# Top-k search of the sparse-attention indexer: whole-number keys for both halves, one chain per query block, bounds of two blocks kept on ScalarE

## The chip, the core and the metric

The kernel runs on one core of one Trainium2 chip. The metric is the device time of one execution in microseconds, the median of several runs. The core's engines are TensorE (PE; PEld is its weight load), VectorE (DVE), ScalarE (ACT), GpSimd (POOL) and SyncE (SP, which issues the DMAs). Each has a queue of its own and works through it in order.

## What is computed

One layer of a decoder trunk over 1024 tokens of width 1024: an embedding norm, two self-attentions side by side (a sliding window of 128, and a sparse attention that lets each query see 256 chosen keys), an output projection, cross-attention to 256 memory tokens and a squared-ReLU feed-forward. The part that matters here is the choice of keys:

```python
dots = jnp.einsum('bqhd,bsd->bqhs', iqb, ik, preferred_element_type=jnp.float32) * (IDX_DIM ** -0.5)
score = jnp.einsum('bqh,bqhs->bqs', iwb.astype(jnp.float32), jax.nn.relu(dots))
causal = key_pos[None, :] <= t[:, None]
score = jnp.where(causal[None], score, NEG_INF)
_, idx = lax.top_k(score, topk)          # topk = 256
```

Ties go to the lowest index. Queries come in blocks of 128, one to a partition; block n has (n + 1) * 128 causal keys, so blocks 0 and 1 take all of theirs and only the six blocks 2 to 7 are searched.

## The kernel before, in words

Matmuls split each fp32 operand into a high and a low part and add three products (`mm3`, L102; every matmul is recorded at L86). The program is written in phases, but a planner sets the order of each engine's queue when the kernel is built, from its own estimates of time, and that order is then fixed. The stretch of this case is phase 1:

- **Scores** (`index_scores`, L572). For each index head and block PE makes the products, ACT applies the relu (L585), DVE adds them up in `sc` (L592). After the last head POOL copies the high 16 bits of each score to `hi_k` (L594).
- **Search** (L606 to L741). The 256th largest score of each query is found bit by bit: 15 bits of the high half (L715), then 16 of the low half among the scores that share the high half (L730). In each bit the keys at or above a bound are counted, and the bound moves. For blocks 2 to 5 DVE counts (`count`, L638, with an accumulator), and its small steps on the four bounds go together as 128x4 (L672, L677 for a high bit; L697, L698, L699 for a low one). For blocks 6 and 7 ACT sums the signs of key minus bound (`sign_sum`, L641, L642), and DVE moves the bound by small 128x1 steps: L668, L672, L677 for a high bit, L692, L693 for a low one. High bounds are bit patterns in int32, compared as bf16; low bounds are whole numbers in fp32. `lo_k` (L711, on POOL) and L718 to L729 (on DVE) stand between the halves.
- **Masks** (L742 to L751). For each block five passes on DVE turn the scores into a mask of 0 and -1e30.
- **Fill** (`fill`, L490 to L550, issued from L754). Beside the search PE makes the projections of queries and keys and the keys and values of the memory tokens. ACT empties the PSUM banks (L393, L456, L465, L487); weights come in by DMA to the ring `wr`, ACT, DVE or POOL make the high part (L160, L158, L156), POOL or DVE the low part (L161). The last units are `mem_v` (two products for each of four heads; ACT L465, then DVE L466) and `mem_vo`.

Phase 2 (attention) needs the fill's results; its first step on DVE that PE waits for in each unit is the split of the transposed probabilities (L783). After that come the output projection, cross-attention and the feed-forward, which the change doesn't touch.

Of the kernel before, what the change touches and what calls it, by code (L numbers as in the profile page):

```python
# [34 lines left out]
def kernel(ctx: ExitStack, tc: tile.TileContext, x, mem, ln_emb_g, ln_emb_b, w_in, b_in,  # L35
# [395 lines left out]
    # memory keys, and memory values taken through the output projection  # L431
# [86 lines left out]
    def first_loads(i):  # L518
        """The first heads' operands, a part at a time, each behind the last load of weights."""
# [52 lines left out]
    def index_scores(j, qs):  # L572
        for e in range(2):
            h = 2 * j + e
            for n in (2, 4, 6, 3, 5, 7):
# [17 lines left out]
                if h == 7:  # L593
                    POOL.tensor_scalar(hi_half(n), halves(n, 1), 1.0, 0.0, op0=OP.mult, op1=OP.add)  # L594
# [23 lines left out]
    h16 = p1.tile([P, NQ], F32)
    base = p1.tile([P, NQ], F32)
    need = p1.tile([P, NQ], F32)  # L620
    t_lo = p1.tile([P, NQ], F32)
    thr = p1.tile([P, NQ], I32)
    junk = {e: p1.tile([P, 1024], BF, name="junk" + e, tag="r", bufs=3) for e in "va"}
    lo_k = {}
    for tag, bufs, ns in (("ikh", 1, (7, 6)), ("ikl", 1, (5, 4, 3)), ("qs", 4, (2,))):
        t = p1.tile([P, sum(n + 1 for n in ns) * P], U16, name="lo_k", tag=tag, bufs=bufs)
        o = 0
        for n in ns:
            lo_k[n] = t[:, o:o + (n + 1) * P]
            o += (n + 1) * P  # L630

# [3 lines left out]
    def hi_f(n):  # L635
        return hi_k[n].bitcast(BF)

    def count(key, c, o, op=OP.is_ge):  # L638
        DVE.tensor_scalar(junk["v"][:, :key.shape[-1]], key, c, None, op0=op, op1=OP.add, accum_out=o)

    def sign_sum(key, c, o):  # L641
        ACT.activation(junk["a"][:, :key.shape[-1]], key, AF.Sign, bias=c, accum_out=o)  # L642

    class Chain:
        def __init__(self, blocks, sign):
            self.b, self.sign, self.k = blocks, sign, len(blocks)
            self.nm = str(blocks[0])
            self.s = slice(blocks[0] - 2, blocks[0] - 2 + self.k)

        def small(self, nm, dt=F32):  # L650
            return p1.tile([P, self.k], dt, name=nm + self.nm, bufs=2)

        def counts(self, keys, c):
            n = self.small("n")
            for i, q in enumerate(self.b):
                (sign_sum if self.sign else count)(keys(q), c[:, i:i + 1], n[:, i:i + 1])
            return n

        # high halves; a ScalarE chain holds -c and compares with c less one place (of a positive c)
        def start_hi(self):  # L660
            self.c = self.small("c", I32)
            DVE.tensor_scalar(self.c, neg_i[:, self.s], (1 << 30) | (-(1 << 31) if self.sign else 0), None, op0=OP.bitwise_xor)

        def bit_hi(self, b):
            c = self.c
            if self.sign:
                c = self.small("d", I32)
                DVE.scalar_tensor_tensor(c, pos_i[:, self.s], (1 << (b + 1)) - 1, self.c, op0=OP.bitwise_and, op1=OP.bitwise_xor)  # L668
            n = self.counts(hi_f, f(c))
            least = 2 * TOPK - (self.b[0] + 1) * P if self.sign else TOPK  # L670
            u = self.small("u", I32)
            DVE.tensor_scalar(u, n, float(least), float(1 << b), op0=OP.is_ge, op1=OP.mult)  # L672
            if b > 16:
                o, x = self.small("c", I32), (1 << b) | (1 << (b - 1))
            else:
                o, x = T_hi[:, self.s], (1 << b) | (-(1 << 31) if self.sign else 0)
            DVE.scalar_tensor_tensor(o, self.c, x, u, op0=OP.bitwise_xor, op1=OP.bitwise_xor)  # L677
            self.c = o

        # low halves, as integers that grow with the score  # L680
        def start_lo(self):
            self.c = self.small("e")
            DVE.memset(self.c, 0.5 - (1 << 15) if self.sign else float(1 << 15))
            if self.sign:
                DVE.tensor_scalar(need[:, self.s], need[:, self.s], 2.0, -float((self.b[0] + 1) * P), op0=OP.mult, op1=OP.add)
# [748 lines left out]
```

## Time and profile before

| | |
|---|---|
| median of 3 runs | 1594.6 us (1593.33 to 1598.8) |
| span of the profiled execution | 1591.6 us; its own time isn't listed apart |
| PE busy | 1452.5 us (91%) |
| DVE busy | 1192.3 us (75%) |
| ACT busy | 782.3 us (49%) |
| POOL busy | 840.3 us (53%) |
| TensorE clock granted, mean | 0.964 of full speed |

A busy share is a mean over stages with different limits: DVE is at 75% of the span, but the stretch of the search has to be read by itself. Durations of neighbouring instructions of one engine overlap by some tens of nanoseconds, so what an instruction costs its engine is best read from one start to the next.

### The profile page before, as it was taken

The page shows a single profiled execution, that of the slowest core. Times are in us where ns is not written, and L with a number is a line of the kernel's source. Part 1 is how long each engine was busy: PE and PEld are TensorE (multiplying, and loading weights), DVE is VectorE, ACT ScalarE, POOL GpSimd, SP SyncE. Part 2 cuts the span into 40 slices and gives each one's busy share as a digit, 9 for nine tenths or more (in the row PEclk, how much of TensorE's full clock was granted, in tenths as well). Part 3 has the DMA queues.
Part 4 walks back from the last instruction along what each step waited for, and adds up shares of the span by engine and source line. Part 5 has one row for each costly group of instructions (what it writes and reads, how often), then busy time and mean ns, then how long its engine had stood idle before and what let it go on. Part 6 is the DMA issues. An engine that isn't in the chain of part 4 may idle for free. (4 is left out here: it accounts for less than half of the span.)

```text
span 1591.6 us, 22193 instructions
## 1 busy us (share of the span) xinstructions
PE 1452.5 (91%) x7190; PEld 1211.1 (76%) x7190; DVE 1192.3 (75%) x2399; ACT 782.3 (49%) x1545; POOL 840.3 (53%) x753
## 2 busy tenths in 40 slices
PE   5989878777999999899999979999999999999887
PEld 4877656666898988678888858888888887888676
DVE  8649999999886886986363496575544799987857
ACT  6336555634787884234434245545455443444422
POOL 6215635635655664765655575645445244443755
PEclk9999889988999999999999989999999999999899
DMA  6252434668559348524323134433333933420002
GB/s 215 79 154 67 118 82 121 175 219 228 170 152 274 111 133 283 174 82 126 107 73 100 40 89 137 130 109 109 124 100 107 385 115 133 129 84 1 27 30 102
DMA packets 139905, 206.62 MB, mean 130 GB/s; under 512 B 18055, under 2 KB 83086, under 8 KB 139790
## 3 DMA queue, kind: packets, MB, share of 16 engines
q1 hardware_dynamic: 139790, 205.21, 41.3%
q8 instruction: 57, 0.93, 0.3%
q14 instruction: 58, 0.48, 0.1%
HBM read 151.66 MB, written 52.45 MB: 128 GB/s over the span
## 5 line engine op out<-in xcount | busy, mean ns | idle before, releaser
L161 POOL TENSOR_TENSOR wl<-wr,wh 128x512 fp32r<-128x512 f32 x158 | 232.7, 1493 | 155.7 <-ACT wh L160 123.9
L86 PE MATMUL b<-a,wh 128*128 128x512 f32 x1072 | 298.4, 400 | 9.6 <-DVE a L1089 8.0
L86 PE MATMUL b<-wl,wh 128*128 128x512 f32 x1192 | 281.2, 396 | 13.8 <-POOL wl L1103 11.6
L86 PEld LDWEIGHTS b<-wl,wh 128*128 128x128 f32 x1192 | 227.1, 191 | 64.9 <-POOL wl L1103 13.8
L86 PEld LDWEIGHTS b<-a,wh 128*128 128x128 f32 x1072 | 202.6, 190 | 58.6 <-issue 8.9
L1103 POOL TENSOR_TENSOR wl<-a,wl 128x512 fp32r<-128x512 f32 x44 | 91.2, 2074 | 114.9 <-ACT wl L1102 108.8
L86 PE MATMUL fill<-xT,wh 128*128 128x512 f32 (+1 forms) x416 | 130.2, 393 | 20.4 <-ACT wt L393 20.4
L160 ACT ACTIVATE wh<-wr 128x512 fp32r<-128x512 f32 x136 | 80.9, 628 | 129.6 <-PE b L86 46.1
L1103 POOL TENSOR_TENSOR wh<-row,wh 128x512 fp32r<-128x512 f32 x72 | 97.4, 1357 | 88.6 <-ACT wh L1102 84.7
L86 PE MATMUL b<-wh,a 128*128 128x512 f32 (+1 forms) x416 | 122.3, 369 | 6.1 <-DVE a L775 4.5
L86 PE MATMUL b<-a,wl 128*128 128x512 f32 x400 | 123.0, 396 | 0.0
L86 PEld LDWEIGHTS fill<-xT,wh 128*128 128x128 f32 x416 | 80.7, 200 | 37.4 <-ACT wt L393 22.1
L1102 ACT ACTIVATE wh<-a 128x512 fp32r<-128x512 f32 x80 | 50.6, 632 | 115.2 <-PE b L86 84.1
L86 PEld LDWEIGHTS b<-wh,a 128*128 128x128 f32 x416 | 76.2, 191 | 21.4 <-DVE a L775 5.0
L1296 DVE TENSOR_TENSOR xr<-xr,b 128x512 f32<-128x512 f32 x132 | 81.5, 677 | 12.9 <-PE b L86 12.9
L86 PEld LDWEIGHTS b<-a,wl 128*128 128x128 f32 x400 | 75.0, 188 | 17.4
L86 PE MATMUL fill<-xT,wl 128*128 128x512 f32 (+1 forms) x208 | 81.4, 393 | 0.0
L1221 DVE TENSOR_TENSOR lt<-b,lt 128x512 f32<-128x512 f32 x80 | 53.4, 686 | 36.2 <-PE b L86 31.3
L783 DVE TENSOR_TENSOR PT<-tr,PT 128x512 fp32r<-128x512 f32 (+3 forms) x128 | 71.0, 575 | 11.2 <-ACT PT L782 10.7
L86 PE MATMUL b<-wl,a 128*128 128x512 f32 (+1 forms) x208 | 76.2, 369 | 2.3 <-POOL wl L161 2.3
L1102 ACT ACTIVATE wh<-row 128x512 fp32r<-128x512 f32 x72 | 45.0, 627 | 62.7 <-PE b L86 49.7
L782 ACT ACTIVATE PT<-tr 128x512 fp32r<-128x512 f32 (+3 forms) x128 | 62.2, 506 | 21.1 <-PE tr L884 13.3
(331 smaller groups left out, 3630.6 us busy)
## 6 DMA issues: line engine op xcount, KB each, us to landing
row<-in_w_up_dram SPq DMA_DIRECT2D x32, 512.0 KB, 4.4
ff_d<-lt SPq DMA_DIRECT2D x28, 512.0 KB, 3.0
a<-in_w_down_dram SPq DMA_DIRECT2D x50, 256.0 KB, 5.3
a<-ff_d SPq DMA_DIRECT2D x46, 256.0 KB, 3.3
wr<-in_xa_wkv_dram SPq DMA_DIRECT2D x32, 256.0 KB, 3.1
wr<-in_w_o_dram SPq DMA_DIRECT2D x32, 256.0 KB, 3.1
wr<-in_xa_wq_dram SPq DMA_DIRECT2D x32, 256.0 KB, 2.7
wr<-vwo_d SPq DMA_DIRECT2D x32, 256.0 KB, 2.8
```

Of the source, the lines that this page charges most:

```text
L86: i = PE.matmul(o, a, b, start=start, stop=stop)
L160: ACT.activation(hs, raw, AF.Copy)
L161: lo[i % len(lo)].tensor_tensor(out=ls, in0=raw, in1=f(hs), op=OP.subtract)
L782: ACT.activation(PT[0], pt, AF.Copy)
L783: DVE.tensor_tensor(out=PT[1], in0=pt, in1=f(PT[0]), op=OP.subtract)
L1102: ACT.activation(hl[:, 0], raw, AF.Copy)
L1103: return lo.tensor_tensor(out=hl[:, 1], in0=raw, in1=f(hl[:, 0]), op=OP.subtract)
L1221: DVE.tensor_tensor(out=o, in0=a, in1=b, op=op)
L1296: DVE.tensor_tensor(out=xs, in0=xs, in1=p, op=op)
```

## The change

Both halves are now searched as whole numbers in fp32 bounds. `to_keys` runs for each block as soon as its scores are complete: DVE counts the scores that aren't negative, makes the block's sign and offsets as 128x1 columns, and POOL writes the high half as signed whole numbers that grow with the score. Every block has a chain of its own: a `Counter` (blocks 2 to 5) counts and moves its bound on DVE in two steps that take the other operand as a per-partition scalar (L665, L667 of the changed kernel), a block's move standing behind the next block's count. A `Signer` (blocks 7 and 6) does all of a bit on ACT: the sum of signs, the sign of that sum, the new bound (L680, L684, L687). After line 561 line numbers of the changed kernel differ from those before; L86 to L561 are the same. Comments are dropped as well. The diff, cut to its core:

```diff
@@ the keys, when a block's scores are complete @@
+    def to_keys(n):
+        new_junk()
+        count(halves(n, 1, I16), 0.0, col(cnt0, n))
+        DVE.tensor_scalar(col(neg, n), col(cnt0, n), float(TOPK), -1.0, op0=OP.is_ge, op1=OP.add)
+        DVE.tensor_scalar(col(flip, n), col(neg, n), 2.0, 1.0, op0=OP.mult, op1=OP.add)
+        POOL.tensor_scalar(hi_half(n), halves(n, 1, I16), col(flip, n), col(neg, n), op0=OP.mult, op1=OP.add)
+        DVE.tensor_scalar(col(least, n), col(neg, n), col(cnt0, n), float(TOPK), op0=OP.mult, op1=OP.add)
+        DVE.tensor_scalar(col(low, n), col(neg, n), -65535.0, None, op0=OP.mult)
...
                 if h == 7:
-                    POOL.tensor_scalar(hi_half(n), halves(n, 1), 1.0, 0.0, op0=OP.mult, op1=OP.add)
+                    to_keys(n)
...
@@ the chains @@
-    class Chain:
...
+    class Counter:
...
+        def look(self):
+            self.got = self.small("n")
+            count(self.key, self.c, self.got)
+
+        def move(self, b):
+            u = self.small("u")
+            DVE.tensor_scalar(u, self.got, self.least, float(1 << b), op0=OP.is_ge, op1=OP.mult)
+            o = self.small("c") if b else self.out
+            DVE.tensor_scalar(o, u, self.c, -float(1 << b) / 2 if b else -1.0, op0=OP.add, op1=OP.add)
+            self.c = o
+
+    class Signer(Counter):
...
+            DVE.tensor_scalar(self.least, least, -2.0, float((n + 1) * P + 1), op0=OP.mult, op1=OP.add)
+
+        def look(self):
+            self.got = self.small("n")
+            ACT.activation(junk_a[:, :self.key.shape[-1]], self.key, AF.Sign, bias=self.c, accum_out=self.got)
+
+        def move(self, b):
+            u = self.small("u")
+            ACT.activation(u, self.got, AF.Sign, bias=self.least)
+            if b:
+                o = self.small("c")
+                ACT.activation(o, u, AF.Identity, scale=-float(1 << b) / 2, bias=self.c)
+                self.c = o
             else:
...
+                DVE.tensor_scalar(self.out, u, 0.5, self.c, op0=OP.mult, op1=OP.subtract)
+
+    def search(keys, least, out, bits):
+        every = [(Signer if n in SIGN else Counter)(n, keys[n], col(least, n), col(out, n), bits) for n in range(NB - 1, 1, -1)]
+        last = None
+        for b in range(bits - 1, -1, -1):
+            for s in every:
+                s.look()
+                if isinstance(s, Signer):
+                    s.move(b)
+                    continue
+                if last is not None:
+                    last[0].move(last[1])
+                last = s, b
+        last[0].move(last[1])
...
+    search(hi_k, least, T_hi, 15)
+    for n in range(NB - 1, 1, -1):
+        count(hi_k[n], col(T_hi, n), col(base, n), OP.is_gt)
+        DVE.scalar_tensor_tensor(lo_k[n], hi_k[n], col(T_hi, n), lo_k[n], op0=OP.is_equal, op1=OP.mult)
+        DVE.tensor_scalar(col(need, n), col(base, n), -1.0, col(least, n), op0=OP.mult, op1=OP.add)
+    search(lo_k, need, t_lo, 16)
...
```

Three places of the queues follow, before and after.

DVE, one bit of the low half, before (`lo_k` and `e` are the keys and bounds, `n` the counts, `u` the step; the number behind `e`, `u` and `n` is a block's, 2 for blocks 2 to 5 together):

```order
L639 TENSOR_SCALAR junkv_1621,n2_2067<-lo_k_1624,e2_2053 128x640
L692 TENSOR_SCALAR u7_2085<-n7_2083,need_1618 128x1
L639 TENSOR_SCALAR junkv_1621,n2_2067<-lo_k_1624,e2_2053 128x768
L693 SCALAR_TENSOR_TENSOR e7_2086<-e7_2064,u7_2085 128x1
L697 TENSOR_TENSOR u2_2072<-n2_2067,need_1618 128x4
L692 TENSOR_SCALAR u6_2101<-n6_2099,need_1618 128x1
L698 SCALAR_TENSOR_TENSOR u2_2072<-u2_2072,e2_2053 128x4
L693 SCALAR_TENSOR_TENSOR e6_2102<-e6_2080,u6_2101 128x1
L699 TENSOR_SCALAR e2_2073<-u2_2072 128x4
```

The same place in the changed kernel (`c` are the bounds):

```order
L584 TENSOR_SCALAR junk_1658,n5_2294<-lo_k_1656,c5_2268 128x768
L665 TENSOR_SCALAR u2_2296<-n2_2276,need_882 128x1
L667 TENSOR_SCALAR c3_2280<-u3_2278,c3_2246 128x1
L584 TENSOR_SCALAR junk_1658,n4_2300<-lo_k_1656,c4_2274 128x640
L665 TENSOR_SCALAR u5_2302<-n5_2294,need_882 128x1
L667 TENSOR_SCALAR c2_2298<-u2_2296,c2_2248 128x1
L584 TENSOR_SCALAR junk_1658,n3_2306<-lo_k_1656,c3_2280 128x512
```

The steps for blocks 6 and 7 have gone from DVE, the four blocks move one by one, and all small steps have the form TENSOR_SCALAR with one tensor operand.

ACT beside the search, before, low half:

```order
L642 ACTIVATE junka_1622,n7_2149<-lo_k_1623,e7_2130 128x1024
L393 ACTIVATE wt_2967<-fill_2942,colst_73 128x512
L642 ACTIVATE junka_1622,n6_2165<-lo_k_1623,e6_2146 128x896
L393 ACTIVATE wt_2978<-fill_2974,zcol_860 128x512
L642 ACTIVATE junka_1622,n7_2171<-lo_k_1623,e7_2152 128x1024
```

ACT in the changed kernel, high half:

```order
L680 ACTIVATE junk_a_1659,n6_1972<-hi_k_1586,c6_1940 128x896
L393 ACTIVATE wt_3237<-fill_3212,colst_73 128x512
L687 ACTIVATE c7_1970<-u7_1968,c7_1934 128x1
L684 ACTIVATE u6_1974<-n6_1972,l6_1671 128x1
L393 ACTIVATE wt_3248<-fill_3244,zcol_860 128x512
L680 ACTIVATE junk_a_1659,n7_2002<-hi_k_1617,c7_1970 128x1024
```

Before, every bound (`e`) that a sum of signs reads comes from DVE; now it (`c`) comes from an ACT instruction a few places ahead in the same queue. The fill's evictions (L393) stand between them in both.

DVE at the search's end, before:

```order
L747 TENSOR_SCALAR r<-sc,thr 128x384
L466 SCALAR_TENSOR_TENSOR wt<-fill,colst,wt 128x256
L639 TENSOR_SCALAR junkv,ngt<-lo_k,t_lo 128x768
L639 TENSOR_SCALAR junkv,ngt<-lo_k,t_lo 128x896
L639 TENSOR_SCALAR junkv,ngt<-lo_k,t_lo 128x1024
L740 TENSOR_TENSOR ngt<-ngt,base 128x6
L741 TENSOR_SCALAR ngt<-ngt 128x6
L748 SCALAR_TENSOR_TENSOR r<-r,ngt 128x384
```

DVE at the search's end in the changed kernel:

```order
L466 SCALAR_TENSOR_TENSOR wt<-fill,colst,wt 128x256
L161 TENSOR_TENSOR wl<-wr,wh 128x512 x2
L690 TENSOR_SCALAR t_lo<-u_2788,c_2754 128x1
L466 SCALAR_TENSOR_TENSOR wt<-fill,colst,wt 128x256 x2
L690 TENSOR_SCALAR t_lo<-u_2793,c_2760 128x1
L161 TENSOR_TENSOR wl<-wr,wh 128x512
L717 TENSOR_TENSOR lo<-t_lo,flip 128x6
L584 TENSOR_SCALAR junk,ngt<-lo_k,t_lo 128x896
```

Of the eight L466, one stood ahead of the first mask step (L747), a second right behind it, the sixth after the masks of three blocks. Now the sixth (the `x2` row holds the fifth and sixth) stands ahead of all mask steps, of which the first (L733) comes 12 rows further on. The first split of probabilities (L769, before L783) stands behind all six masks in both.

## Rows read from the trace of the kernel before

**Rows 1.** Busy time by stage (columns: stretch, length, five engines, clock, DMA, GB/s).

```profile
core 0: us, PE busy (x) PEld busy (x) DVE busy (x) ACT busy (x) POOL busy (x), PEclk, DMA share, GB/s
...
163.20:251.70 88.50, 71.27 (x284) 56.37 (x283) 88.04 (x277) 48.17 (x84) 46.94 (x47) 0.88 0.39 106
251.70:343.30 91.60, 69.42 (x397) 60.63 (x395) 88.74 (x258) 54.05 (x98) 48.96 (x44) 0.91 0.65 194
343.30:398.70 55.40, 37.44 (x191) 30.61 (x192) 51.91 (x78) 21.45 (x48) 26.39 (x22) 0.84 0.65 187
398.70:440.00 41.30, 38.79 (x275) 35.53 (x273) 33.02 (x122) 32.20 (x87) 27.34 (x45) 0.97 0.58 174
```

**Rows 2.** What PE waited for, 163.2 to 343.3 us: total, times, longest.

```profile
PE fill L86 <- ACT wt L393: 26.7, 8, 7.0
```

**Rows 3.** ACT, same stretch, by line: busy us, mean ns, idle before, what ended it.

```profile
L642 ACT ACTIVATE junka<-lo_k,e 128x896 bf16<-128x896 uint16 (+1 forms) x32 | 35.0, 1094 | 35.6 <-DVE e L693 26.9 <-DVE lo_k L724 5.0 <-DVE u L697 3.0
L642 ACT ACTIVATE junka<-hi_k,d 128x896 bf16<-128x896 bf16 (+1 forms) x30 | 32.8, 1095 | 30.5 <-DVE d L668 15.4 <-DVE u L672 12.9 <-DVE c L677 2.1
```

**Rows 4.** Small steps on DVE, same stretch, by line: busy us, mean ns.

```profile
L677 DVE SCALAR_TENSOR_TENSOR c<-c,u 128x1 int32<-128x1 int32 (+1 forms) x42 | 13.1, 325 | 0.0
L668 DVE SCALAR_TENSOR_TENSOR d<-pos_i,c 128x1 int32<-128x1 int32 x29 | 9.4, 323 | 0.0
L693 DVE SCALAR_TENSOR_TENSOR e<-e,u 128x1 f32<-128x1 f32 x30 | 9.0, 300 | 0.0
L698 DVE SCALAR_TENSOR_TENSOR u<-u,e 128x4 f32<-128x4 f32 x16 | 6.9, 431 | 0.2
```

**Rows 5.** Shortest, median and longest of such steps, in ns.

```profile
L693 DVE SCALAR_TENSOR_TENSOR e<-e,u x30: 145/156/1236, 249.2 to 320.2; 128x1 f32<-128x1 f32 x30
L699 DVE TENSOR_SCALAR e<-u x15: 155/170/1228, 256.2 to 337.8; 128x4 f32<-128x4 f32 x15
L692 DVE TENSOR_SCALAR u<-n,need x32: 194/208/215, 248.3 to 325.9; 128x1 f32<-128x1 f32 x32
```

**Rows 6.** POOL, 163.2 to 343.3 us, by line: its tensor-tensor work.

```profile
L396 POOL TENSOR_TENSOR wt<-wt 128x512 fp32r<-128x512 f32 x25 | 33.5, 1344 | 1.5
```

**Rows 7.** DVE in order of time, one bit (start, duration).

```profile
256.43 0.61 DVE L639 TENSOR_SCALAR_CACHE_REDUCE junkv<-lo_k,e 128x384 bf16<-128x384 uint16 x1
...
259.74 0.21 DVE L692 TENSOR_SCALAR u<-n,need 128x1 f32<-128x1 f32 x1
...
260.45 0.61 DVE L639 TENSOR_SCALAR_CACHE_REDUCE junkv<-lo_k,e 128x384 bf16<-128x384 uint16 x1
```

**Rows 8.** ACT, whole span, by form: a short exponential, an accumulator read.

```profile
L877 ACT ACTIVATE wt<-wt,sm 128x128 f32<-128x128 f32 x8 | 3.2, 398 | 1.1 <-DVE sm L874 1.1
...
L642 ACT ACTIVATION_READ_ACCUMULATOR junka<-lo_k,e 128x1 f32 x32 | 6.0, 188 | 0.0
```

**Rows 9.** ACT in order of time: an instruction and the next, which reads its output.

```profile
984.71 0.72 ACT L1114 ACTIVATE lt<-lt,colst 128x512 f32<-128x512 f32 x1 [2.25 <-DVE lt L1221]
985.46 0.63 ACT L1115 ACTIVATE lt<-lt 128x512 f32<-128x512 f32 x1
```

**Rows 10.** DVE in order of time, from the search's end.

```profile
356.92 0.68 DVE L161 TENSOR_TENSOR wl<-wr,wh 128x512 fp32r<-128x512 f32 x1
...
372.23 0.86 DVE L466 SCALAR_TENSOR_TENSOR wt<-fill,colst,wt 128x256 fp32r<-128x256 f32 x2
...
398.74 0.42 DVE L783 TENSOR_TENSOR PT<-tr,PT 128x256 fp32r<-128x256 f32 x1 [1.20 <-ACT PT L782]
```

**Rows 11.** ACT in order of time, what feeds the L466 pair of 372.23 us.

```profile
358.37 0.63 ACT L160 ACTIVATE wh<-wr 128x512 fp32r<-128x512 f32 x1 [8.59 <-DMA wr<-in_xa_wkv_dram]
...
366.41 0.90 ACT L465 ACTIVATE wt<-fill,colst 128x256 fp32r<-128x256 f32 x2 [1.65 <-PE fill L86]
```

**Rows 12.** DVE, 343.3 to 398.7 us, by line: the costliest mask pass, the fill's last step.

```profile
L748 DVE TENSOR_TENSOR_SCAN r<-r,ngt 128x384 f32<-128x384 f32 (+5 forms) x6 | 12.1, 2010 | 0.1
...
L466 DVE SCALAR_TENSOR_TENSOR wt<-fill,colst,wt 128x256 fp32r<-128x256 f32 x7 | 3.3, 477 | 0.3 <-ACT wt L465 0.3
```

More of the change, by code (lines that the diff above doesn't have):

```diff
@@ L630 @@
             o += (n + 1) * P
+    new_junk()
+    junk_a = p1.tile([P, 1024], BF, name="junk_a", tag="r", bufs=3)
     def srow(n):
         return sc[:, SCO[n]:SCO[n] + (n + 1) * P]
[L635 to L642, printed above, removed]
@@ L644 @@
-    class Chain:
[L645 to L674, printed above, removed]
-            else:
[L676 to L685, printed above, removed]
-        def bit_lo(self, b):
-            n = self.counts(lo_k.get, self.c)
-            u = self.small("u")
-            o = self.small("e") if b else t_lo[:, self.s]
-            if self.sign:
-                DVE.tensor_scalar(u, n, need[:, self.s], -float(1 << b), op0=OP.is_ge, op1=OP.mult)
-                DVE.scalar_tensor_tensor(o, self.c, float(1 << b) / 2 if b else 0.5, u, op0=OP.add, op1=OP.add)
-                if not b:
-                    DVE.tensor_scalar(o, o, -1.0, None, op0=OP.mult)
-            else:
-                DVE.tensor_tensor(out=u, in0=n, in1=need[:, self.s], op=OP.is_ge)
-                DVE.scalar_tensor_tensor(u, u, float(1 << b), self.c, op0=OP.mult, op1=OP.add)
-                DVE.tensor_scalar(o, u, -float(1 << b) / 2 if b else -1.0, None, op0=OP.add)
-            self.c = o
@@ L702 @@
-    for n in range(2, NB):
-        count(hi_k[n].bitcast(I16), 0.0, cnt0[:, n - 2:n - 1])
-    DVE.tensor_scalar(neg, cnt0, float(TOPK), -1.0, op0=OP.is_ge, op1=OP.add)
-    DVE.tensor_copy(neg_i, neg)
-    DVE.tensor_scalar(pos_i, neg_i, -1, None, op0=OP.bitwise_xor)
-    DVE.tensor_scalar(flip[:, 0], neg, 2.0, 1.0, op0=OP.mult, op1=OP.add)
-    DVE.tensor_scalar(flip[:, 1], neg, -65535.0, None, op0=OP.mult)
-    for n in range(2, NB):
-        i = n - 2
-        POOL.tensor_scalar(lo_k[n], halves(n, 0), flip[:, 0, i:i + 1], flip[:, 1, i:i + 1], op0=OP.mult, op1=OP.add)
@@ L730, with __init__, small @@
-    for b in range(15, -1, -1):
-        for ch in chains:
-            ch.bit_lo(b)
-    lo = p1.tile([P, NQ], F32)
-    DVE.tensor_tensor(out=lo, in0=t_lo, in1=flip[:, 0], op=OP.mult)
-    DVE.tensor_tensor(out=thr, in0=lo, in1=flip[:, 1], op=OP.add)
-    DVE.tensor_tensor(out=thr, in0=thr, in1=T_hi, op=OP.bitwise_or)
+    class Counter:
+        def __init__(self, n, key, least, out, bits):
+            self.n, self.key, self.least, self.out, self.bits = n, key, least, out, bits
+            self.c = self.small("c")
+            DVE.memset(self.c, float(1 << bits - 1))
+        def small(self, nm):
+            return p1.tile([P, 1], F32, name=nm + str(self.n), bufs=2)
+        def look(self):
[7 more added lines that the diff above has]
+            self.c = o
@@ new lines @@
+    for n in range(2, NB):
+        POOL.tensor_scalar(lo_k[n], halves(n, 0), col(flip, n), col(low, n), op0=OP.mult, op1=OP.add)
+    search(hi_k, least, T_hi, 15)
[4 more added lines that the diff above has]
+    search(lo_k, need, t_lo, 16)
@@ L737 @@
+    thr = p1.tile([P, NQ], I32)
+    hi_i = p1.tile([P, NQ], I32)
+    lo = p1.tile([P, NQ], F32)
+    DVE.tensor_tensor(out=lo, in0=t_lo, in1=flip, op=OP.mult)
+    DVE.tensor_tensor(out=thr, in0=lo, in1=low, op=OP.add)
+    DVE.tensor_tensor(out=lo, in0=T_hi, in1=flip, op=OP.mult)
+    DVE.tensor_tensor(out=lo, in0=lo, in1=neg, op=OP.add)
+    DVE.tensor_scalar(hi_i, lo, 65536.0, None, op0=OP.mult)
+    DVE.tensor_tensor(out=thr, in0=thr, in1=hi_i, op=OP.bitwise_or)
     ngt = p1.tile([P, NQ], F32)
@@ L738 @@
     for n in range(2, NB):
-        count(lo_k[n], t_lo[:, n - 2:n - 1], ngt[:, n - 2:n - 1], OP.is_gt)
-    DVE.tensor_tensor(out=ngt, in0=ngt, in1=base, op=OP.add)
-    DVE.tensor_scalar(ngt, ngt, -float(TOPK), -NEG, op0=OP.add, op1=OP.mult)
+        count(lo_k[n], col(t_lo, n), col(ngt, n), OP.is_gt)
+    DVE.tensor_tensor(out=ngt, in0=ngt, in1=need, op=OP.subtract)
+    DVE.tensor_scalar(ngt, ngt, -NEG, None, op0=OP.mult)
     for n in range(2, NB):
```

53 lines of the change are left out of this document (18 added, 35 removed).

## The prediction

> **What bounds the kernel now.** I read the busy times by stage first [rows 1]. In the search, 163.2 to 343.3 us, DVE is busy 88.04 of 88.50 and 88.74 of 91.60 us, while PE is busy 71.27 and 69.42 at a granted clock of 0.88 and 0.91. In the masks, to 398.7 us, DVE is busy 51.91 of 55.40 and PE 37.44. Behind that PE is busy 38.79 of 41.30 at 0.97. So up to 398.7 us the end is set by DVE, and after it by PE. PE's queue behind the masks is the same in both kernels, so what the first split of probabilities (L783, 398.74 us [rows 10]) gains or loses I carry to the end one to one.
>
> The second view is of waits. PE waits 26.7 us in the search, in 8 pieces, for one releaser, ACT's eviction L393 [rows 2]. ACT itself is idle 35.6 + 30.5 = 66 us ahead of its sums of signs, nearly all of it until DVE hands over a bound [rows 3]. That is a chain DVE, ACT, PE: an eviction is queued behind a sum of signs that waits for a small step on DVE, which stands behind counts. The third view is of the small steps. L677, L668, L693 and L698 have means of 0.300 to 0.431 us [rows 4], but a median of 0.156 to 0.170 where I looked, with single ones of 1.23 us [rows 5]. That is about the length of a POOL tensor-tensor, mean 1.344 [rows 6]; I take it that these two-operand steps wait while POOL works. L692, which has one tensor and a per-partition scalar, never did: 194 to 215 ns in 32 of 32 [rows 5].
>
> **DVE's search.** Removed are the small steps of before, those of blocks 6 and 7 and those of 128x4; added are two per bit for each of four blocks, 31 bits x 8 = 248, all in the form of L692. An undisturbed bit goes from 256.43 to 260.45, 4.02 us, and the six small steps at its end take 260.45 - 259.74 = 0.71, 0.12 each [rows 7]. That bit has eight of them in all, about 0.96 us; the new one has eight as well, about 1.0. So the number of steps saves nothing, and only the blocking counts. At 0.17 us for an undisturbed step (the longest of the medians [rows 5]) the excess is 42 x 0.155 + 29 x 0.153 + 30 x 0.130 + 16 x 0.261 = 6.5 + 4.4 + 3.9 + 4.2 = 19 us [rows 4], and 31 more 128x4 steps (L697, L699) add an estimated 5. So 24 us go if no new step is blocked. Between the halves some eight small steps go (the casts and products of 128x6), an estimated 1 us. `to_keys` adds some 26 small steps of 0.12, 3 us, less 1 that the old preparation took; its POOL pass replaces L594's copy. The last moves, with no count behind them, cost an estimated 0.5. Sum: -24 - 1 + 2 + 0.5 = about **-23 us**; DVE's search ends near 320 instead of 343.
>
> Here a rule of the Trainium skill speaks against the change. By the row, L692 is never held up [rows 5], and the sum of 248 steps uses that. The Trainium skill, page "SBUF — State Buffer", section "Who interferes with whom", says that DVE and GpSimd share a pair of ports as an exclusive lock, that a DVE instruction with two SBUF inputs contends for it, and that `tensor_scalar` without a written-out accumulator can contend too where its operands allow a two-port mode. The first part agrees with L693 and L698; by the last the new steps would be no safer than the old, and that is a rival below.
>
> **ACT.** It loses its waits for DVE and gets two 128x1 instructions for each of two blocks in each of 31 bits, 124. No row of before has that form. Below stands the accumulator read, 0.188 us, above the shortest exponential with a pointer operand, 128x128 at 0.398 [rows 8]. I take the middle, 0.29, because a 128x1 moves less than the one and has more operands than the other: 124 x 0.29 = 36 us (23 to 49). A following instruction that reads the output starts 985.46 - 984.71 - 0.72 = 0.03 us after the first ends [rows 9], so the chain itself adds little. ACT is busy about 102 us of 180 now, so about 138 of 157 then. It hides all of this beside DVE until the room of 157 - 102 = 55 us, plus what the end lets slip, is used: with 180 us to go the point is 78 / 124 = 0.63 us each. The cover is the 66 us in which it waited. If it were gone, the evictions would be late, and PE's L393 waits would stay.
>
> The Trainium skill would leave this work on DVE: its page "ScalarE: Activation LUTs", section "Rules for kernel authors", keeps adds and multiplies off ScalarE. Its figure in "What ACT_TABLE_LOAD costs" (a fixed 280 ns with a pointer bias) gives an estimate of 35 us for the 124, beside the 36 above. On rows DVE is full and ACT idle, so 124 steps kept on DVE would lengthen its path by 124 x 0.12 = 15 us, which is the sum without this part.
>
> **The masks and the gate.** Here most of the doubt lies. DVE's order of before puts the sixth L466 (one of the pair at 372.23 us [rows 10]; its start is t6 below) behind the masks of three blocks; the new order puts it ahead of all masks. So the masks now wait for the fill: L466 waits for ACT's L465, that for PE's `mem_v`, that for split weights, and everything up to the first L783 is queued behind it. Where does that sixth L466 fall? In before its L465 ran at 366.41 after 1.65 us of waiting for PE, and L160 ahead of it at 358.37 after 8.59 us for a weight transfer [rows 11]; that transfer waited for a ring slot that DVE's L161 freed at 356.92 + 0.68, 0.8 us earlier [rows 10], behind masks. In the new queue these L161 come right at the search's end, near 320. From L160's end (359.0) to L465's end (367.3) it is 8.3 us, and with the L161 itself and the transfer, some 2 us, ahead of it the sixth L466 cannot come before 320 + 10.5 = 331 us. From the other side: 366.4 less PE's 26.7 us of L393 waits [rows 2] is 340, or 346 if a quarter of these remain; of the rest of PE's work some moves earlier as the clock of 0.84 rises [rows 1]. I take **335 us**, range 331 to 343, nearer the lower end because the waits of both L393 and L161 go.
>
> What DVE must do from there to the first split: of the 51.91 us in the masks' stretch [rows 1] all but some 3 of L466's 3.3 [rows 12] and 2.7 of L161 stay, 46, plus gaps of 55.40 - 51.91 = 3.5 and about 1.5 of other steps that come behind: 51 us. The costliest passes, L748 at 12.1 us in six, don't change [rows 12]. So the first split comes at 335 + 51 = 386, against 398.74: a gain of 12.7, from which 1594.6 - 12.7 = **1582 us**. Of DVE's 23 us about 10 are lost at the gate. The sum is made on one profiled execution: its span is 1591.6 us, 3.0 below the median of the runs shown, and its own time isn't listed; I apply the difference to the median. With t6 from 331 to 343 the first split is at 382 to 394, so 1578 to 1590.
>
> **The rivals.**
> 1. *The gate holds the masks back.* If the sixth L466 comes later than 398.7 - 51 = 348, every further us is lost. If PE's `mem_v` came as late as today (372), the first split would be at 423, 24 us later: 1619, slower. For it: PE is busy 78% of the search, and the fill is a long chain of weights, evictions and ring slots, of which only the L393 waits fall away. Against: 26.7 us of waits go, and PE idles 40 us in the search [rows 1, 2]. Chance 0.18, of which 0.11 lies within 0.3% (a gate of 343 to 352) and 0.07 above.
> 2. *The new steps are blocked by POOL too.* With the mean excess of L699, (330 - 170) ns, on 248 steps they pay 40 us against the 24 that go [rows 5]: DVE's path grows by 13 to 17 us, and the time is about 1608, slower. L692 speaks against it, 32 of 32. Chance 0.04. The Trainium skill's rule above would allow it.
> 3. *ACT becomes the bound*, from 0.63 us for each small step: at 0.75 it would be busy 102 + 93 = 195 us, 15 more than the stage has; 1610. Against: [rows 8]. Chance 0.03.
> 4. *The blocking only moves*: POOL's work holds up other two-operand steps (L161, the products before the low half) and DVE's end stays, 1595. Chance 0.03.
> 5. *No loss at the gate*: PE is there when DVE is, and the first split gains 18 to 23: 1572 to 1577. For it speaks the clock; against it, the 10.5 us from L161 to L466. Chance 0.10.
>
> **How the numbers follow.** The forecast has 0.62, rival 5 has 0.10: faster 0.72. Same is 0.11 + 0.03 = 0.14, slower 0.07 + 0.04 + 0.03 = 0.14. The bound is 0.3%, 4.8 us, which is about what a measurement of this kernel can tell from no change. The range reaches from 1572 (the whole of DVE's 23 us) to 1596 (a gate of 349); left out are the slower cases and a part of the small ones, less than 0.2.
>
> **What would show it.** In the changed kernel's profile L665 and L667 should have means of 0.16 to 0.21 us with none above 0.3; one above 1 us would be rival 2. ACT's idle time ahead of L680 should fall from 66 us to under 15 and its 128x1 steps read 0.2 to 0.4 us. PE's waits for L393 should shrink from 26.7 to under 8. DVE's last count should end near 320, the sixth L466 near 335 with DVE idle some 10 us ahead of it for L465, and the first L769 (the old L783) near 386. If DVE idles more than 25 us ahead of that L466, rival 1 holds. The prediction is wrong if the first L769 moves and the end doesn't move with it: then PE's stage behind 398.7 us isn't as full as [rows 1] says.

## The result and the profile after

| | before | changed |
|---|---|---|
| median | 1596.7 us (4 runs, 1593.33 to 1601.59) | 1576.26 us (4 runs, 1572.76 to 1579.26) |
| ratio | | 0.9869 [0.9848, 0.9891] |
| span of the profiled execution | 1591.6 us | 1572.0 us |
| first split of probabilities on DVE | 398.74 us | 384.65 us |

The changed kernel is faster by 20 us. A later measurement of the same kernel (e10 below) gave 0.9905 [0.9884, 0.9925], 16 us; the intervals overlap by a little. 1582 had been forecast, with a range of 1572 to 1596.

Busy time by stage of the changed kernel (stretch, length, PE, PEld, DVE, ACT, POOL, clock, DMA), cut at its own marks; [rows 1] is the same view of before:

```profile
163.20:251.70 88.50, 82.25 (x356) 66.68 (x356) 84.39 (x318) 67.92 (x173) 58.24 (x62) 0.96 0.50 139
251.70:326.00 74.30, 58.36 (x345) 51.58 (x344) 73.87 (x249) 51.07 (x124) 41.19 (x35) 0.87 0.68 211
326.00:346.20 20.20, 17.88 (x86) 13.93 (x86) 8.48 (x18) 14.13 (x31) 10.89 (x9) 0.88 0.80 274
346.20:384.60 38.40, 22.89 (x129) 20.25 (x127) 37.46 (x71) 12.95 (x39) 24.33 (x23) 0.75 0.53 141
384.60:426.00 41.40, 37.06 (x248) 33.95 (x249) 31.92 (x114) 29.80 (x78) 21.75 (x37) 0.91 0.59 168
```

PE now does 82.25 us of work in the first stretch where it did 71.27. DVE is all but full in the search and in the masks, with a hole between: 8.48 of 20.20 us. The small steps of DVE, by line (shortest/median/longest in ns), answer to [rows 4, 5]:

```profile
L667 DVE TENSOR_SCALAR c<-u,c x116: 195/203/209, 169.5 to 316.4; 128x1 f32<-128x1 f32 x116
L665 DVE TENSOR_SCALAR u<-n,need x64: 200/204/215, 243.0 to 319.0; 128x1 f32<-128x1 f32 x64
L665 DVE TENSOR_SCALAR u<-n,least x60: 200/209/216, 168.5 to 229.5; 128x1 f32<-128x1 f32 x60
```

None of them is held up: the longest took 216 ns. ACT, 150 to 330 us, by line (busy us, mean ns, idle before and what ended it), answers to [rows 3, 8]; under it PE's waits in the same stretch, which answer to [rows 2]:

```profile
L680 ACT ACTIVATE junk_a<-hi_k,c 128x1024 bf16<-128x1024 int16 (+1 forms) x30 | 33.1, 1102 | 5.6 <-POOL hi_k L595 5.6
L680 ACT ACTIVATE junk_a<-lo_k,c 128x1024 bf16<-128x1024 uint16 (+1 forms) x30 | 32.6, 1086 | 11.4 <-DVE lo_k L711 11.4
L684 ACT ACTIVATE u<-n,l 128x1 f32<-128x1 f32 x59 | 17.3, 293 | 0.1
L687 ACT ACTIVATE c<-u,c 128x1 f32<-128x1 f32 x56 | 16.4, 293 | 0.0
```

```profile
PE fill L86 <- DVE wl L161: 9.0, 6, 2.6
PE fill L86 <- ACT wt L393: 6.8, 4, 4.9
```

The idle time ahead of the sums of signs fell from 66 to 17 us, none of it for a bound, and PE's wait for L393 from 26.7 to 6.8 (its wait for DVE's L161 rose from 5.5 to 9.0). DVE in order of time at the search's end, which answers to [rows 10]:

```profile
319.07 0.34 DVE L667 TENSOR_SCALAR t_lo<-u,c 128x1 f32<-128x1 f32 x2
...
323.42 2.25 DVE L161 TENSOR_TENSOR wl<-wr,wh 128x512 fp32r<-128x512 f32 x2
334.86 0.21 DVE L690 TENSOR_SCALAR t_lo<-u,c 128x1 f32<-128x1 f32 x1 [9.18 <-ACT u L684]
337.80 0.88 DVE L466 SCALAR_TENSOR_TENSOR wt<-fill,colst,wt 128x256 fp32r<-128x256 f32 x2 [2.72 <-DMA vwo_d<-wt]
...
346.22 0.42 DVE L733 TENSOR_SCALAR r<-sc,thr 128x384 f32<-128x384 f32 x1
...
384.65 1.21 DVE L769 TENSOR_TENSOR PT<-tr,PT 128x256 fp32r<-128x256 f32 x3
```

DVE's own chains end at 319.4 us. Then it idles 9.18 us, not for the fill but for L684: ScalarE's chain for block 7 isn't done. Why it is late is seen in ACT's order of time between the halves:

```profile
223.69 0.30 ACT L684 ACTIVATE u<-n,l 128x1 f32<-128x1 f32 x1
234.74 1.15 ACT L680 ACTIVATE junk_a<-lo_k,c 128x1024 bf16<-128x1024 uint16 x1 [10.76 <-DVE lo_k L711]
```

ScalarE has finished its high half at 223.99 and waits 10.76 us until DVE makes the low keys of block 7, for which its queue has no place before its own high half ends.

### The profile page after: what moved, and what is told of

Its sections match the earlier page's. It is cut to its first block, busy times and chain, and to the rows that moved or that the text cites. A ratio compares the mean times of both kernels' runs of the same rounds, so it can differ in the third digit from the quotient of the medians.

```text
span 1572.0 us, 22293 instructions
## 1 busy us (share of the span) xinstructions
PE 1449.3 (92%) x7190; PEld 1208.9 (77%) x7190; DVE 1165.3 (74%) x2442; ACT 798.3 (51%) x1665; POOL 847.4 (54%) x753
## 5 line engine op out<-in xcount | busy, mean ns | idle before, releaser
L86 PE MATMUL b<-a,wh 128*128 128x512 f32 x1072 | 300.2, 402 | 8.8 <-DVE a L1075 8.1
L161 POOL TENSOR_TENSOR wl<-wr,wh 128x512 fp32r<-128x512 f32 x158 | 228.5, 1466 | 145.8 <-ACT wh L160 137.4
L86 PE MATMUL b<-wl,wh 128*128 128x512 f32 x1192 | 278.1, 393 | 13.5 <-POOL wl L1089 13.3
L86 PEld LDWEIGHTS b<-wl,wh 128*128 128x128 f32 x1192 | 224.9, 189 | 63.9 <-POOL wl L1089 16.3
L86 PEld LDWEIGHTS b<-a,wh 128*128 128x128 f32 x1072 | 203.5, 191 | 58.2 <-issue 8.9
L160 ACT ACTIVATE wh<-wr 128x512 fp32r<-128x512 f32 x136 | 81.1, 627 | 128.5 <-PE b L86 46.4
L86 PE MATMUL fill<-xT,wh 128*128 128x512 f32 (+1 forms) x416 | 126.8, 384 | 6.8 <-ACT wt L393 6.8
L86 PE MATMUL b<-wh,a 128*128 128x512 f32 (+1 forms) x416 | 122.5, 369 | 7.6 <-DVE a L761 5.6
L86 PE MATMUL b<-a,wl 128*128 128x512 f32 x400 | 123.0, 396 | 0.0
L86 PEld LDWEIGHTS fill<-xT,wh 128*128 128x128 f32 x416 | 78.5, 195 | 23.0 <-ACT wt L393 8.3
L86 PEld LDWEIGHTS b<-wh,a 128*128 128x128 f32 x416 | 76.4, 191 | 22.8 <-DVE a L761 5.9
L1282 DVE TENSOR_TENSOR xr<-xr,b 128x512 f32<-128x512 f32 x132 | 81.5, 675 | 14.1 <-PE b L86 14.1
L86 PEld LDWEIGHTS b<-a,wl 128*128 128x128 f32 x400 | 75.0, 188 | 17.4
L86 PE MATMUL fill<-xT,wl 128*128 128x512 f32 (+1 forms) x208 | 79.8, 385 | 0.0
L1100 ACT ACTIVATE lt<-lt,colst 128x512 f32<-128x512 f32 x60 | 43.2, 722 | 68.1 <-DVE lt L1207 67.3
L86 PE MATMUL b<-wl,a 128*128 128x512 f32 (+1 forms) x208 | 76.2, 369 | 1.3 <-POOL wl L161 1.3
L769 DVE TENSOR_TENSOR PT<-tr,PT 128x512 fp32r<-128x512 f32 (+3 forms) x128 | 70.6, 576 | 8.7 <-ACT PT L768 8.4
```

The lines of the kernel that those rows point to most:

```text
L86: i = PE.matmul(o, a, b, start=start, stop=stop)
L160: ACT.activation(hs, raw, AF.Copy)
L161: lo[i % len(lo)].tensor_tensor(out=ls, in0=raw, in1=f(hs), op=OP.subtract)
L769: DVE.tensor_tensor(out=PT[1], in0=pt, in1=f(PT[0]), op=OP.subtract)
L1100: ACT.activation(c, src, AF.Relu, bias=colst[:, C_UP + col:C_UP + col + 1])
L1282: DVE.tensor_tensor(out=xs, in0=xs, in1=p, op=op)
```

## The experiments

All ratios are against the kernel before, measured on the same chip. "First split" is the first L769 in the profiled execution (398.74 us before), wherever its line number has moved.

| run | median us | ratio | first split us |
|---|---|---|---|
| changed | 1576.26 | 0.9869 [0.9848, 0.9891] | 384.65 |
| e10, changed again | 1579.67 | 0.9905 [0.9884, 0.9925] | 386.26 |
| e1, bounds on DVE | 1578.14 | 0.9890 [0.9848, 0.9931] | 386.86 |
| e11, e1 again | 1582.98 | 0.9912 [0.9889, 0.9934] | 386.78 |
| e2, two operands | 1598.08 | 1.0011 [0.9989, 1.0033] | 404.46 |
| e3, e1 and e2 | 1601.42 | 1.0038 [1.0018, 1.0058] | 411.44 |
| e4, more on ACT | 1595.45 | 0.9998 [0.9973, 1.0023] | 401.92 |
| e5, masks first | 1577.89 | 0.9879 [0.9852, 0.9905] | 385.86 |
| e6, low half early | 1575.50 | 0.9862 [0.9837, 0.9887] | 378.55 |
| e7, e5 and e6 | 1571.07 | 0.9840 [0.9810, 0.9870] | 377.36 |
| e8, e5 and own junk | 1569.68 | 0.9820 [0.9776, 0.9864] | 376.98 |
| e9, e7 and own junk | 1570.09 | 0.9826 [0.9780, 0.9872] | 376.14 |
| e12, e9 and bounds on DVE | 1577.03 | 0.9885 [0.9865, 0.9904] | 384.85 |

### Which part made the gain

**e2_two_operands.** One line. The queues of ACT and POOL keep their order. On DVE, against what was expected, the planner also moved some other steps (L442, L158, L161, L466) by a few places among the counts:

```diff
-            DVE.tensor_scalar(o, u, self.c, -float(1 << b) / 2 if b else -1.0, op0=OP.add, op1=OP.add)
+            DVE.scalar_tensor_tensor(o, u, -float(1 << b) / 2 if b else -1.0, self.c, op0=OP.add, op1=OP.add)
```

> Edit: the second step of a move of blocks 2 to 5 (L667) is a SCALAR_TENSOR_TENSOR with two tensor operands instead of a TENSOR_SCALAR with one and a per-partition scalar; same numbers, same order of every queue. Theory 1 (a small step with two tensor operands waits while POOL works): the 124 L667 rise from a mean of 0.20 to between 0.30 and 0.43 us, with single ones above 1.2, VectorE's counts end 12 to 20 us later than 319, and as VectorE had 9 us to spare at the end of the search the first split comes 4 to 12 us later: 1580 to 1588. Theory 2 (the old steps were slow because of int32 or their 128x4 form): L667 stays under 0.22 us and the time within 1573 to 1579.

DVE's small steps in e2, 163.2 to 343.3 us, by line (busy us, mean ns):

```profile
L667 DVE SCALAR_TENSOR_TENSOR c<-u,c 128x1 f32<-128x1 f32 x116 | 47.6, 410 | 0.0
L665 DVE TENSOR_SCALAR u<-n,need 128x1 f32<-128x1 f32 x64 | 13.0, 204 | 0.0
```

L667 rose from a mean of 0.20 to 0.41 us, L665 beside it stayed, DVE's chains end at 338.4 instead of 319.4, and the whole gain is gone: ratio 1.0011. Three stretches of e2, DVE and under it POOL, in order of time:

```profile
170.10 6.09 DVE L667 SCALAR_TENSOR_TENSOR c<-u,c 128x1 f32<-128x1 f32 x1
...
200.17 0.20 DVE L665 TENSOR_SCALAR u<-n,least 128x1 f32<-128x1 f32 x1
200.30 1.13 DVE L667 SCALAR_TENSOR_TENSOR c<-u,c 128x1 f32<-128x1 f32 x1
...
202.15 0.14 DVE L667 SCALAR_TENSOR_TENSOR c<-u,c 128x1 f32<-128x1 f32 x1
202.21 0.60 DVE L584 TENSOR_SCALAR_CACHE_REDUCE junk<-hi_k,c 128x384 bf16<-128x384 int16 x1
```

```profile
170.01 1.19 POOL L707 TENSOR_SCALAR lo_k<-sc,flip,low 128x1024 uint16<-128x1024 uint16 x1
171.17 2.54 POOL L161 TENSOR_TENSOR wl<-wr,wh 128x512 fp32r<-128x512 f32 x2
173.66 2.51 POOL L396 TENSOR_TENSOR wt<-wt 128x512 fp32r<-128x512 f32 x2
176.30 0.62 POOL L395 TENSOR_SCALAR wt<-wt 128x512 fp32r<-128x512 f32 x1
...
200.13 1.29 POOL L396 TENSOR_TENSOR wt<-wt 128x512 fp32r<-128x512 f32 x1
```

The L667 of 200.30 ends at 201.43, the POOL instruction that began before it at 201.42. The one of 170.10 ends at 176.19, when five POOL instructions that follow each other without a gap have ended (173.66 + 2.51 = 176.17). At 202.15 POOL is idle, and the same step takes 0.14. The rest of the 124 L667 go the same way: none of the 66 that began with POOL idle took over 0.2 us, 50 of the other 58 did, and all but the one of 170.10 ended within 0.03 us of the POOL instruction in which they had begun. In the changed kernel 117 of the 248 steps began with more than 0.3 us of a POOL instruction left, and none took over 0.22. So a 128x1 step with two tensor operands waits while POOL works; one with a per-partition scalar beside its tensor doesn't. Theory 1 holds.

e2 leaves the width at one column. A step of before shows that the width counts too, first DVE, then POOL:

```profile
282.84 0.56 DVE L699 TENSOR_SCALAR e<-u 128x4 f32<-128x4 f32 x1
282.75 0.62 POOL L395 TENSOR_SCALAR wt<-wt 128x512 fp32r<-128x512 f32 x1
```

L699 has one tensor operand as well, but is 128x4. Three of its 16 began with more than 0.3 us of a POOL instruction left, and all three waited for its end. The changed kernel's steps are 128x1.

Off was the size at the first split, 20 us instead of 4 to 12, because I took DVE's 9 us of idle time as room. It isn't: DVE's later end of the high half also makes ACT wait 20.8 us instead of 10.8 for its low keys, and DVE then waits for ACT as long as before:

```profile
353.77 0.21 DVE L690 TENSOR_SCALAR t_lo<-u,c 128x1 f32<-128x1 f32 x1 [9.17 <-ACT u L684]
```

**e1_bounds_on_dve.** The two moves of `Signer` go to DVE:

```diff
-            ACT.activation(u, self.got, AF.Sign, bias=self.least)
+            DVE.tensor_scalar(u, self.got, self.least, -float(1 << b) if b else 1.0, op0=OP.is_ge, op1=OP.mult)
...
-                ACT.activation(o, u, AF.Identity, scale=-float(1 << b) / 2, bias=self.c)
+                DVE.tensor_scalar(o, u, self.c, float(1 << b) / 2, op0=OP.add, op1=OP.add)
```

> Edit: the two moves of blocks 7 and 6 in each bit go from ScalarE to VectorE, as two TENSOR_SCALAR steps with a per-partition scalar; everything else as in the changed kernel. Theory 1 (moving the bounds to ScalarE is worth its price): VectorE gets 124 small steps of 0.125 us start to start, 15.5 us, so its counts end near 335 instead of 319 us; ScalarE loses 124 x 0.19 = 23 us of work but waits for VectorE again, more than 40 us in all ahead of its sums of signs; the first split comes 5 to 12 us later than 384.6 and the time is 1581 to 1588. Theory 2 (in the changed kernel ScalarE is the later of the two and VectorE waits 9.2 us for it at the end, so the moves are on the wrong engine): same or faster than the changed kernel, 1568 to 1577.

DVE's chains end at 336.3 instead of 319.4 us, and ACT waits for it again: in 150 to 345 us

```profile
ACT junk_a L680 <- DVE c L687: 37.7, 38, 5.6
```

Yet the first split is only 2.2 us later, and the times can't be told apart. **e11_bounds_on_dve_again** put it beside **e10_changed_again** on one chip.

> The changed kernel as it is, five rounds beside the next two on one chip, as the measure for them: 1573 to 1579.

> The kernel of e1_bounds_on_dve, five rounds on the chip of e10. Theory 1 (keeping the bounds on ScalarE gains the 2.3 us by which the first split is earlier, 384.6 against 386.9): 1 to 4 us slower than e10. Theory 2 (it gains nothing): within 1 us or faster.

0.9905 [0.9884, 0.9925] against 0.9912 [0.9889, 0.9934], first splits 386.26 and 386.78: no difference that could be measured. What DVE saves by the bounds on ACT, it waits for ACT at the end. e10's median of 1579.67 lies above what was expected.

**e3_both.** 

> Both of the last edits: ScalarE's moves on VectorE and L667 of blocks 2 to 5 with two tensor operands. If both parts made the gain, VectorE's counts end at 319 + 15.5 + 12 to 20, near 350, the first split comes 15 to 25 us later than 384.6, and the time is 1591 to 1601, about that of the kernel before. If the gate (the fill's sixth L466 ahead of the masks) sets the first split and not VectorE, under 1586.

1601.4 us and a first split 26.8 us later than 384.6, both just beyond what was expected: without the two parts the new form of the search is slower than the old by 0.4%. With e2 this says that the one-operand form carries the gain, and that the parts don't add: behind e2, moving the bounds to DVE costs 7 us at the first split (411.44 against 404.46).

### What holds the end of the search

**e4_more_on_act.** Two copies go into each chain of blocks 7 and 6 in each bit, ahead of the sign (L684); they do no part of the search.

```diff
+            v = self.small("u")
+            ACT.activation(v, self.got, AF.Identity, bias=zcol)
+            g = self.small("u")
+            ACT.activation(g, v, AF.Identity, bias=zcol)
-            ACT.activation(u, self.got, AF.Sign, bias=self.least)
+            ACT.activation(u, g, AF.Sign, bias=self.least)
```

> Edit: two more 128x1 ACTIVATE (copies) in the chain of each of blocks 7 and 6 in each bit, 124 in all, about 0.19 us each start to start, 23 us. Theory 1 (ScalarE's queue is now what ends the search, as the wait of 9.2 us of VectorE for it says): its last sum of signs comes 12 to 23 us later than 335, VectorE's wait for it grows to 20 to 32 us, and the time is 1586 to 1598. Theory 2 (that end is set by the weight transfers that ScalarE's splits wait for, and its own work fits between): the added work falls into the waits for transfers (11.8 us) and for the low keys (11.4 us), and the time is under 1580.

```profile
370.34 0.21 DVE L694 TENSOR_SCALAR t_lo<-u,c 128x1 f32<-128x1 f32 x1 [10.74 <-ACT u L688]
```

L694 is L690 of before the edit. It comes 35 us later than 334.86, more than the 23 us added, though the copies took up most of ACT's wait for its low keys (2.3 us instead of 11.4); where the rest comes from isn't shown in full. Its own wait is 10.7 instead of 20 to 32, since the planner has put steps of attention ahead of it (they come to idle there, too). The time, 1595.5, is as theory 1 had it, the waits are not: work added to ScalarE's queue lengthens the path that ends the search, and 124 more small steps cost the kernel the whole gain.

**e5_masks_first.** Thresholds and masks in two groups, and L690 ordered behind the mask of block 3:

```diff
+    for ns in ((2, 3, 4, 5), (6, 7)):
+        g = slice(ns[0] - 2, ns[-1] - 1)
+        for end in pending if ns[0] == 6 else ():
+            tc.add_manual_dep(end().ins, masked[1].ins.name, NOSYNC, reason="order")
+        DVE.tensor_tensor(out=lo[:, g], in0=t_lo[:, g], in1=flip[:, g], op=OP.mult)
...
```

> Edit to the changed kernel: thresholds and masks are made in two groups, blocks 2 to 5 and blocks 6 and 7, and the last step of blocks 7 and 6 (L690 of the low half), for which VectorE waited 9.2 us, stands in its queue behind the masks of blocks 2 and 3. Theory 1 (VectorE's work up to the first split is what is left of the stage, and its idle time of 9.2 + 2.7 us at the end of the search is lost): some 10 us of masks fill that time, the first split comes 6 to 10 us ahead of 384.6 and the time is 1566 to 1571. Theory 2 (the fill's L466 and L161, which these masks now stand ahead of, hold PE and with it the end): no gain, 1573 to 1580.

No gain, but for a reason that neither theory had:

```profile
337.98 1.02 DVE L746 TENSOR_TENSOR_SCAN r<-r,ngt 128x384 f32<-128x384 f32 x1 [10.17 <-ACT junk_a L682]
```

The first mask's scan is ready, and waits 10.17 us for ACT's last sum of signs. It writes a tile of the ring `r`, in which `junk_a` lies, the tile that takes the signs themselves and that nobody reads.

**e8_masks_first_own_junk.** `junk_a` goes into room beside the low keys of block 2.

```diff
-    junk_a = p1.tile([P, 1024], BF, name="junk_a", tag="r", bufs=3)
+    junk_a = t[:, 3 * P:3 * P + 1024].bitcast(BF)
```

> e5_masks_first with ScalarE's junk tile moved out of the ring that the mask tiles (r) take, into free room beside the low keys of block 2. In e5 the first mask's scan stood idle for 10.2 us until ScalarE's last sum of signs gave the ring slot back. Theory 1 (that slot alone took the gain): the idle time goes, the first split comes 6 to 10 us ahead of e5's 385.9, and the time is 1566 to 1572. Theory 2 (the fill's weights, behind masks now, hold VectorE and PE in its place): VectorE idles as long at an L466 or L161 of the fill, 1573 to 1580.

```profile
328.00 1.02 DVE L746 TENSOR_TENSOR_SCAN r<-r,ngt 128x384 f32<-128x384 f32 x1
...
376.98 0.42 DVE L781 TENSOR_TENSOR PT<-tr,PT 128x256 fp32r<-128x256 f32 x1
```

The same scan stands at 328.00 without a wait, the first split comes 8.9 us ahead of e5's, and the time is 1569.7: theory 1. (The planner's order of PE also moves beyond the search here, so not every microsecond need be the slot's.)

**e6_low_half_early.** 

> Edit to the changed kernel: VectorE prepares the low keys of blocks 7 and 6 (count, product, need) one bit earlier, ahead of the last high bit of blocks 2 to 5, instead of behind it; nothing else moves. Theory 1 (ScalarE's chain ends the search, and it starts its low half late): its wait of 11.4 us for L711 falls to 5 to 8 us, its last sign comes 3 to 5 us earlier, and as much goes from VectorE's wait of 9.2 us: 1571 to 1574. Theory 2 (ScalarE's end is set by the weight transfers that its splits wait for): the time gained is waited out at the next transfer, 1574.5 to 1579.

ACT's wait for the low keys fell from 11.4 to 6.5 us, DVE's for L684 from 9.2 to 3.3, and the first split came 6.1 us earlier. The median, 1575.5, lies 0.8 us under the changed kernel's and 4.2 under e10's, with intervals that overlap: by the trace theory 1, by the times alone unclear.

**e7_both_orders.** 

> Both edits of order together. Theory 1: VectorE's idle time at the end of the search goes almost wholly, first split 8 to 12 us ahead of 384.6, time 1564 to 1569. Theory 2 (the fill holds the end): not under 1572.

1571.1, first split 7.3 us earlier: a little short of theory 1 in both, and under theory 2's 1572 by less than the runs differ (1566.4 to 1575.6). **e9_both_orders_own_junk** takes the last idle time.

> e7_both_orders with ScalarE's junk tile moved in the same way. VectorE idled 2.5 us for that slot in e7 and 0.9 for L465. Theory 1: the first split comes 2 to 3 us ahead of e7's 377.4, time 1564 to 1570. Theory 2 (nothing left to gain there, the masks and the fill's steps fill VectorE): within 1 us of e7's first split, 1568 to 1573.

First split 1.2 us ahead of e7's, 1570.1: nearer to theory 2. DVE in the last 56 us ahead of the first split is busy for 55.46:

```profile
320.00:376.00 56.00, 38.38 (x208) 32.95 (x207) 55.46 (x105) 26.50 (x67) 30.69 (x29) 0.84 0.66 187
```

By their medians e8 and e9 are the fastest versions; between them and e7 nothing is settled, as the intervals overlap.

**e12_best_order_bounds_on_dve.** 

> e9_both_orders_own_junk (masks of blocks 2 and 3 early, low half of blocks 7 and 6 early, ScalarE's junk tile apart) with the bounds of blocks 7 and 6 on VectorE. Theory 1 (with ScalarE's lateness filled by masks, VectorE's 124 x 0.125 = 15.5 us of added steps lie in full on the path): first split 10 to 16 us behind that of e9 (376), 1579 to 1586. Theory 2 (ScalarE's waits still decide): within 4 us of e9, 1566 to 1574.

First split 8.7 us behind e9's, 1577.0, ratio 0.9885 [0.9865, 0.9904] against 0.9826 [0.9780, 0.9872]; the trace goes theory 1's way with a smaller price than 10 to 16, the time lies between the two, and the intervals, taken on two chips, just overlap. So by the trace the bounds on ScalarE are worth something, but only in an order that has other work for DVE while ScalarE finishes; by the times this isn't settled.

## Why the prediction was right, point by point

1. *The form of the small steps.* 24 us were to go from DVE's search if no new step is blocked. None of the 248 was (longest 216 ns), and the chains ended at 319.4 us, forecast 320. e2 shows that the form is the cause: with number type and width as they were, two tensor operands bring the waits back. That the width doesn't matter can't be said, as L699 shows. The Trainium skill, page "SBUF — State Buffer", section "Who interferes with whom", has DVE instructions with two SBUF inputs contend with GpSimd: the trace of e2 agrees. The rule of the Trainium skill's page for `tensor_scalar`, which rival 2 would have reach the new steps, shows on none of the 248 at 128x1; the waits of L699 at 128x4 fit it. Two slips change little: a low bit of before has seven small steps, not eight (112 in 16 bits; the bit that was read holds three L692), so that some 2 us of added steps are missing from the sum, and rival 2's 13 to 17 us give 1608 to 1612.
2. *ACT's steps.* 0.29 us was taken from the middle of two far rows, 0.293 measured; 0.18 from start to start where neighbours belong to different chains, 0.33 where one reads the other's output (L684 at 236.01, L687 at 236.34). The evictions came early and PE's L393 waits fell to 6.8, as forecast. ACT's idle time ahead of L680 is 17 us, forecast under 15, and its cause had not been foreseen: the 10.76 us between the halves.
3. *The gate: the size was right, the mechanism wrong.* I put the sixth L466 at 335 us and said that DVE would idle some 10 us ahead of it for the fill's L465. It came at 338.2, after 9.18 + 2.72 us of idle time. But 9.18 of these are a wait for L684 of ScalarE's chain. The other 2.72 (put down to a store there; in e10 the same place names L465, with 2.6) lie in ScalarE's queue as well: L465 itself had nothing to wait for, but stood behind the last sum of signs (334.72) and a split:

```profile
336.63 0.63 ACT L160 ACTIVATE wh<-wr 128x512 fp32r<-128x512 f32 x1 [0.78 <-DMA wr<-in_xa_wo_dram]
337.29 0.84 ACT L465 ACTIVATE wt<-fill,colst 128x256 fp32r<-128x256 f32 x2
```

So ScalarE's queue set the gate, and not PE's `mem_v`. The 51 us of work behind it were 384.65 - 338.2 = 46.4. The counts of blocks 2 to 5 (3.6 us) now stand ahead of the wait, and the masks' five passes took 30.9 us instead of 37.0 (32.0 in e10), though the sum had the costliest unchanged; more steps of attention between them took a part of this back. The largest piece, before and changed:

```profile
L750 DVE SCALAR_TENSOR_TENSOR r<-r 128x384 f32<-128x384 f32 (+5 forms) x6 | 8.6, 1426 | 0.0
L736 DVE SCALAR_TENSOR_TENSOR r<-r 128x384 f32<-128x384 f32 (+5 forms) x6 | 5.6, 940 | 0.0
```

Why they got cheaper is not shown. A gate 3 us late and 5 us less work behind it made 384.65 out of a forecast of 386: that the two errors cancel is luck.

4. *ScalarE's bounds.* The step that failed: "124 steps kept on DVE would lengthen its path by 124 x 0.12 = 15 us, which is the sum without this part". e1 and e11 show 2.2 and 0.5 us at the first split and none in the time. DVE's path does grow, by 17 us (336.3 against 319.4), but then it has no ScalarE to wait for. I treated rival 3 (ScalarE as the bound) by its busy sum, with a threshold of 0.63 us a step. A queue that is not full can still be last when it begins late (10.76 us) and waits for weights on the way (11.8 us).
5. *Carried one to one.* The first split gained 14.1 us, the span 19.6. Along PE's queue the lead is 14.4 us at 470 us, 16.5 to 16.8 between 590 and 930, 15.7 up to 1310, and then 19.5 within 28 us. That last piece lies in the feed-forward, before and changed, where both do the same work:

```profile
1300.00:1345.00 45.00, 41.99 (x175) 33.32 (x174) 42.57 (x63) 16.11 (x28) 22.13 (x12) 0.96 0.35 117
```

```profile
1284.00:1326.00 42.00, 40.60 (x179) 32.96 (x178) 42.00 (x64) 16.47 (x30) 23.02 (x12) 1.00 0.38 126
```

Of its 3.8 us, 1.5 are waits of PE for split weights (2.9 us before, 1.4 changed); the rest comes with a granted clock of 1.00 instead of 0.96. In e10, with the waits of before and a clock of 1.00, that piece is 1.6 us, and the span is shorter than before by 13.8 in all, with a first split 12.5 earlier. So what can be laid to the change is some 13 to 16 us; the rest of the measured 20 I can't place. Nor is the first split an exact mark against the kernel before: in e2 it comes 5.7 us later than before, yet the span is 1.1 us shorter. The median of 1576.26 lies in rival 5's band (1572 to 1577), but rival 5 isn't what happened: it had the first split gain 18 to 23 us. e10's 1579.67 lies in the forecast's own.

## What to carry to other kernels

Where GpSimd works beside VectorE, give VectorE's small steps the form of one tensor and a per-partition scalar, one column wide: here that alone was worth the whole change, and the same sum written with two tensors took it back. Work moved to an engine with idle time helped here, by the trace, only when the engine that gave it up had something else in its queue meanwhile: look for what the receiving chain waits for at its start, and order the giver's queue for it. And before reordering, look which ring a scratch tile lies in: an output that nobody reads held the next stage for 10 us in e5.

## What the hardware showed that was not expected

- A 128x1 step of 0.14 us stood 6.09 us behind five POOL instructions in a row (170.10 to 176.19 in e2), and one in e3 4.53 us behind four. These are exceptions: 28 other steps of e2 began in a POOL instruction that the next followed without a gap, and each got its turn at the end of the first, as this one, above the two POOL instructions:

```profile
181.06 1.14 DVE L667 SCALAR_TENSOR_TENSOR c<-u,c 128x1 f32<-128x1 f32 x1
180.89 1.30 POOL L161 TENSOR_TENSOR wl<-wr,wh 128x512 fp32r<-128x512 f32 x1
182.15 1.29 POOL L161 TENSOR_TENSOR wl<-wr,wh 128x512 fp32r<-128x512 f32 x1
```

  Why two waited longer is open.
- POOL's TENSOR_SCALAR holds such steps up as well as its TENSOR_TENSOR: in e2 the step of 179.76 took 0.58 us and ended with POOL's L156 (179.73, 0.62 us).
- Undisturbed, the two-operand step is the cheaper one: 0.06 us from its start to the next (202.15 to 202.21) and 148 ns by the median, against 0.12 and 203 ns for the step with a per-partition scalar. The gain is in what it doesn't wait for.
